# Layer 1's projections with norm statistics and one sine table in PSUM, and tokens normed in places of their own

## The chip, the core and the metric

The kernel runs on one core of a Trainium2 chip. Its engines work side by side, each through its own instruction queue in order: TensorE (PE in the profile; PEld is its weight load) multiplies and transposes, VectorE (DVE) and ScalarE (ACT) work element by element and can read and write PSUM, GpSimd (POOL) works on SBUF only, and SyncE (SP) issues most of the DMAs. The metric is the device time of one execution in microseconds.

## What is computed

Two layers over 2048 tokens of width 1024, all in float32. Layer 0 is a mixer with two kinds of banded attention. The change is in layer 1 (and in when one preparation for it is done):

```python
def odd_layer(x, norm_g, w_in, w_out, qn, kn, lq1, lk1, lq2, lk2, subln_g, cos, sin, lambda_init):
    h = rms_norm(x, norm_g)
    proj = h @ w_in
    q, k, v, gate = jnp.split(proj, [C_QK, 2 * C_QK, 2 * C_QK + C_W], axis=-1)
    q = rms_norm(q.reshape(b, s, C_HEADS, 2, HEAD_DIM), qn)
    k = rms_norm(k.reshape(b, s, C_HEADS, 2, HEAD_DIM), kn)
    q1 = apply_rope(q[:, :, :, 0], cos, sin)
...
    o = differential_attention(q1, q2, k1, k2, v, lam)
    o = rms_norm(o, subln_g) * (1.0 - lambda_init)
    y = (o.reshape(b, s, C_W) * jax.nn.silu(gate)) @ w_out
    return x + y
```

`rms_norm` divides by the root of the mean square and multiplies by a gain; `apply_rope` turns each head's two halves of 32 by an angle that depends on the position.

## The kernel before

A float32 product is made of three matmuls: each factor is split into a high part (a ScalarE copy to the matmul's rounded type) and a low part (the remainder, by VectorE or GpSimd), and high x high, high x low and low x high are added in PSUM (names ending in H and L).

`project1` makes queries, keys and values of layer 1 by quarters, with seven products of 256 x 256 squares in place of eight. `PRODUCTS` names them: some multiply quarters of the hidden tokens with quarters of the weights, others sums of quarters (s1 to s4 of the tokens, and sums of the weights that `weight_sums` made while layer 0 ran and stored in the DRAM tensor `t`). Three PSUM accumulators per block hold them: X runs through products 0, 2, 3 and 4 and is copied out after each (tiles a, b, c, d of the pool `xp`), Y holds product 1, Z products 5 and 6; VectorE adds Y and Z to the copied tiles.

The tokens come in two halves of two blocks of 512 (blocks 3 and 2, then 0 and 1). In each half run six groups of 512 columns: values, two of queries, two of keys, values. `steps` gives the order in a group: 14 steps, seven products for each of two blocks (`bi` 0 and 1). In query and key groups both blocks follow each other within a product; in value groups block 1 trails by `LAG` products. A step is 2 x 4 x 3 = 24 matmuls (L759).

Around a step:
- `operand` (L511 to L518) loads one square of weights (`ws`, L514), splits it on ScalarE (L516) and GpSimd (L517) into places of `wp`; `fetch` calls it ahead of use, `gate_weights` eight more times for the gate.
- `hidden` (L536 to L606) is a generator that makes a block: for each of two pairs of token tiles it loads them (L550), squares (L552), takes the inverse root with `rstd` (L197 to L210), scales (L556), transposes on TensorE (L562), splits and adds the quarters (L566 to L599). Tokens, their raw sums and the tiles a to d share the places of the tag `x`.
- `normed` (L627 to L649) norms one quarter of queries or keys of both blocks: squares on ScalarE (L631), a sum on VectorE (L633), `rstd` (ScalarE's Ln and Exp at L204 and L205, four small VectorE operations at L206 to L209), a product (L635), the two sine products on VectorE (L641), and the cosine product and the sum on GpSimd (L645, L649).
- `turn` (L651 to L661) transposes a normed quarter (L656), empties it from PSUM on ScalarE (L658) and VectorE (L659) and stores both parts. Eight turns of a group are spread over the following steps by `later` and `tick`.
- `tables` (L616 to L625) loads cosines and sines of the half's positions and multiplies them with the gains by `rope_tables` (L177 to L195), four tables in SBUF.

The places: PSUM has eight banks, two for transposes (`ptr`) and six for products (`pmm`). In SBUF there are 8 places for weight parts (four pairs), 3 each for the two split results (`ep`), and 6 for `x`. The program's order is a priority: the order of each engine's queue is fixed at build time by a scheduler that plays the program through a model of the engines and takes what is ready first, so an instruction can stand in its queue far ahead of its place in the program.

At the start of the first half the whole of block 3 is made before the first step, block 2 beside the first steps (the generator is advanced after steps of block 0 in group 0). At the change of halves the first new block is begun after the last step of `bi` 0 in the last group, the second beside the next group's first steps.

In layer 0, `project0` runs a round of `weight_sums` per block and group, from the second group of the first half on: a load, four GpSimd operations (L463) and a store, 24 rounds.

Of the kernel before, what the change touches and what calls it, by code (L numbers as in the profile page):

```python
# [10 lines left out]
F32 = mybir.dt.float32  # L11
F32R = mybir.dt.float32r
AF = mybir.ActivationFunctionType
# [19 lines left out]
def f32(ap):  # L33
    return ap.bitcast(F32)
# [52 lines left out]
class Trunk:  # L87
# [88 lines left out]

    def rope_tables(self, pool, gain, scale, tag, nt=S // P):  # L177
        nc = self.nc
        C = pool.tile([P, nt, HD], F32, tag=tag + "C", name=tag + "C")
        Sn = pool.tile([P, nt, HD], F32, tag=tag + "S", name=tag + "S")  # L180

# [43 lines left out]
    def project0(self, es):  # L225
# [166 lines left out]
        for half in range(2):  # L392
# [12 lines left out]
            for gi, (kind, c0, width, o) in enumerate(groups):  # L405
# [4 lines left out]
                for bi, b in enumerate(blocks):  # L410
                    if half or gi:
                        next(sums, None)
# [72 lines left out]
    def project1(self, es):  # L485
# [12 lines left out]
        tq = pool("tq", 2)  # L498
        ep = pool("e", 3)
        sums[0][1] = pool("s1a", 1)  # L500
        gn = pool("g", 1)
        st = pool("st", 3)
        wp = pool("w", 8)
        sums[0][4] = pool("s4a", 1)
        xp = pool("x", 6)
        ptr = pool("ptr", 2, space=PSUM)
        pmm = pool("pmm", 6, space=PSUM)
        mm = nc.tensor.matmul
# [25 lines left out]
        nc.sync.dma_start(gain, a["od_norm"].to_broadcast([P, D]))  # L534

        def hidden(b, i, h):  # L536

# [6 lines left out]

            for p in range(2):
                xs, ss = [], sm.tile([P, 2], F32, tag="xss", name=n + "xss")
                for e in range(2):
                    t = b * NTB + 2 * e + p
                    xt = xp.tile([P, D], F32, tag="x", name=n + "xt")
                    nc.sync.dma_start(xt, x[t * P:(t + 1) * P, :])  # L550
                    junk = tq.tile([P, D], F32, tag="tq", name=n + "junk")
                    nc.scalar.activation(junk, xt, AF.Square, accum_out=ss[:, e:e + 1])  # L552
                    xs.append(xt)
                r = self.rstd(sm, ss, 2, 1.0 / D, n + "x")
                for e in range(2):
                    nc.vector.scalar_tensor_tensor(xs[e], xs[e], r[:, e:e + 1], gain, ALU.mult, ALU.mult)  # L556

                def turned(e, q):
# [11 lines left out]
                def of(k, part):  # L570
                    return S_[k]["HL".index(part)][:, :, p * P:(p + 1) * P]
# [25 lines left out]
                for k in (2, 3, 1, 4):  # L597
                    nc.scalar.activation(of(k, "H"), raws[k], AF.Copy)
                    nc.gpsimd.tensor_tensor(of(k, "L"), raws[k], f32(of(k, "H")), ALU.subtract)  # L599
                yield  # L600
            if b:
# [14 lines left out]
        def tables(blocks):  # L616
# [6 lines left out]
            self.cos, self.sin = (t.rearrange("p r b j d -> p (r b j) d") for t in (cos, sin))  # L623
            tabs["q"] = self.rope_tables(tb, self.gain["od_q_norm"], 0.125, n + "tq", 8)
            tabs["k"] = self.rope_tables(tb, self.gain["od_k_norm"], 1.0, n + "tk", 8)  # L625

        def normed(C, r, tab):  # L627
# [3 lines left out]
            nc.scalar.activation(sq, C.rearrange("p t c -> p (t c)"), AF.Square)  # L631
            ss = sm.tile([P, 16], F32, tag="qss", name=n + "qss")
            nc.vector.tensor_reduce(ss, sq.rearrange("p (h d) -> p h d", d=HD), AX.X, ALU.add)  # L633
            rs = self.rstd(sm, ss, 16, 1.0 / HD, n + "q")
            nc.vector.tensor_tensor(v, v, rs.unsqueeze(2).to_broadcast([P, 16, HD]), ALU.mult)  # L635
# [31 lines left out]
        halves_ = [(3, 2), (0, 1)]  # L667
        LAG = 2

# [34 lines left out]
        h = [{}, {}]  # L704
        making = [hidden(halves_[0][0], 0, h[0]), hidden(halves_[0][1], 1, h[1])]
        for _ in making[0]:
            pass
        making = making[1:]
        tables(halves_[0])
        for _ in range(3):  # L710
            fetch()

        for half, blocks in enumerate(halves_):
            for gi, (kind, g, o) in enumerate(groups):
                T, ps, done = {}, {}, set()
                if kind == "qk":
                    next(gates, None)

                def tile_(nm):
# [24 lines left out]
                for si, (p, bi) in enumerate(steps(half, gi)):  # L744
# [7 lines left out]
                    if opens:  # L752
                        ps[bank, bi] = pmm.tile([P, 2, Q], F32, tag="mm", name=n + "mm" + bank)
                    acc = ps[bank, bi]
# [34 lines left out]
                    tick()  # L789
                    if half == 0 and gi == len(groups) - 1 and bi == 0 and p == self.ORDERS[0][-1]:  # L790
                        nxt = [{}, {}]
                        making = [hidden(halves_[1][i], i, nxt[i]) for i in range(2)]
                        next(making[0])
                    elif half == 0 and gi == len(groups) - 1 and len(making) == 2:
                        next(making[0], None)
                    if gi == 0 and bi == 0 and making:
                        if next(making[0], 0) == 0:
                            making.pop(0)
                if half == 0 and gi == len(groups) - 1:
                    for _ in making.pop(0):  # L800
                        pass
                    h = nxt
                    tables(halves_[1])
        while later:
# [787 lines left out]
```

## Time and profile before

| | us |
|---|---|
| median of three executions | 2926.62 |
| lowest and highest | 2919.79 and 2930.2 |
| the profiled execution | 2917.79 |
| its span, first to last instruction | 2916.0 |

All durations are from the profiled execution. In its views a row of a stretch has its bounds, its length, busy time and number of instructions of each engine, the granted TensorE clock (1.00 is full), and the DMA share with GB/s. A row of a group has line, engine, operation, output and inputs, shapes and count, then busy us and mean ns, then the idle time before and what ended it. A row of waits has total us, number and longest. A row of the timeline has start, duration, engine and line. The page in 40 slices of 73 us (busy tenths; layer 1's projections are slices 17 to 26):

```profile
PE   6999999999899999697978998899999999999998
DVE  8763285347778773449863787359887787776772
POOL 6764254335445454367755777336676666777661
PEclk9999999999999999799998999999999999999999
```

### The profile page before, as it was taken

Reading aid. Unit: us, or ns where it says so; the run is one execution under the profiler, and the core shown is the slowest. Engines: PE = TensorE matmul, PEld = TensorE weight load, DVE = VectorE, ACT = ScalarE, POOL = GpSimd, SP = SyncE. Lnnn points to the kernel's source line nnn. Section 1 sums busy time; section 2 is a strip of 40 time slices with the busy share of each in tenths; the row PEclk is TensorE's granted clock in tenths of the full one; section 3 lists DMA queues with packets and bytes.
Section 4 is the critical chain, followed back from the end, with each engine's and each line's share of the span. In section 5 each row is a group of like instructions: output and inputs, shape, how many; then the busy total and the mean of one; then the engine's idle time right before and its main releaser. Section 6 shows DMA issues by size and latency. Waiting matters only on the chain. (4 is left out here: it accounts for less than half of the span.)

```text
span 2916.0 us, 47395 instructions
## 1 busy us (share of the span) xinstructions
PE 2696.0 (92%) x15112; PEld 2248.2 (77%) x15112; DVE 1933.4 (66%) x4436; ACT 1680.0 (58%) x4011; POOL 1651.3 (57%) x1603
## 2 busy tenths in 40 slices
PE   6999999999899999697978998899999999999998
PEld 5788887888788888597977998677676777676676
DVE  8763285347778773449863787359887787776772
ACT  4443544367767673443434444458897787776761
POOL 6764254335445454367755777336676666777661
PEclk9999999999999999799998999999999999999999
DMA  7897348737877675455655455997868675555442
GB/s 227 288 329 252 110 153 269 236 114 236 234 203 193 181 201 163 156 180 157 203 197 174 152 188 190 236 265 196 242 194 232 183 227 183 141 174 146 145 152 91
DMA packets 420521, 568.03 MB, mean 195 GB/s; under 512 B 44720, under 2 KB 219568, under 8 KB 420272
## 3 DMA queue, kind: packets, MB, share of 16 engines
q1 hardware_dynamic: 411568, 556.61, 63.3%
q10 hardware_dynamic: 8704, 8.39, 0.9%
q8 instruction: 120, 1.97, 0.3%
q14 instruction: 129, 1.06, 0.1%
HBM read 394.21 MB, written 170.66 MB: 194 GB/s over the span
## 5 line engine op out<-in xcount | busy, mean ns | idle before, releaser
L1247 ACT ACTIVATE cP<-cS,cnm 128x512 f32<-128x512 f32 (+3 forms) x640 | 393.8, 620 | 146.4 <-DVE cnm L1244 119.3
L1244 DVE TENSOR_REDUCE cnm<-cS 128x1 f32<-128x512 f32 (+3 forms) x640 | 373.9, 601 | 50.7 <-PE cS L1241 44.2
L1280 POOL TENSOR_TENSOR cP<-cP,cP 128x512 f32<-128x512 f32 (+1 forms) x320 | 356.8, 1143 | 30.8 <-ACT cP L1278 29.7
L1279 POOL TENSOR_SCALAR cP<-cP,crl,cel 128x512 f32<-128x512 f32 (+3 forms) x288 | 206.7, 730 | 239.6 <-DVE crl L1261 134.2
L1296 PE MATMUL cO<-cpt,cv 128*128 128x512 f32 (+3 forms) x640 | 290.7, 541 | 5.9 <-DVE cpt L1294 4.4
L517 POOL TENSOR_TENSOR p1wL<-p1ws,p1wH 128x1024 fp32r<-128x1024 f32 x92 | 227.4, 2476 | 104.2 <-ACT p1wH L516 94.6
L1240 PE MATMUL cS<-ck,cqd 128*128 128x512 f32 (+3 forms) x640 | 262.7, 414 | 14.8 <-DMA ck<-kH 6.4
L1294 DVE COPY cpt<-ctr 128x512 f32<-128x512 f32 (+1 forms) x320 | 190.8, 605 | 121.0 <-PE ctr L1292 118.1
L292 POOL TENSOR_TENSOR p0wL<-p0ws,p0wH 128x512 fp32r<-128x512 f32 (+1 forms) x140 | 170.6, 1244 | 170.8 <-ACT p0wH L290 162.2
L215 PE MATMUL p0mm<-p0wH,p0hH 128*128 128x512 f32 (+1 forms) x640 | 238.9, 376 | 8.6 <-ACT p0vt L447 7.2
L217 PE MATMUL p0mm<-p0wH,p0hL 128*128 128x512 f32 (+1 forms) x640 | 238.6, 373 | 2.8 <-DVE p0hL L318 2.8
L216 PE MATMUL p0mm<-p0wL,p0hH 128*128 128x512 f32 (+1 forms) x640 | 238.3, 373 | 0.0
L1241 PE MATMUL cS<-ck,cql 128*128 128x512 f32 (+3 forms) x640 | 232.5, 368 | 2.0 <-DMA cql<-qL 2.0
L1292 PEld LDWEIGHTS ctr<-ident,cP 128*128 128x128 f32 x1088 | 138.8, 142 | 120.2 <-issue 63.7
L1278 ACT ACTIVATE cP<-cP,cc 128x512 f32<-128x512 f32 (+1 forms) x320 | 189.4, 651 | 26.1 <-DVE cc L1264 24.9
L1292 PE MATMUL ctr<-ident,cP 128*128 128x128 f32 x1088 | 176.9, 276 | 4.1 <-ACT csq L1325 2.6
L759 PE MATMUL p1mmX<-p1wH,p1hH 128*128 128x256 f32 x576 | 168.1, 292 | 8.6 <-ACT p1hH L567 6.1
L516 ACT ACTIVATE p1wH<-p1ws 128x1024 fp32r<-128x1024 f32 x92 | 96.4, 1056 | 125.8 <-PE p1mmX L759 48.7
L759 PE MATMUL p1mmX<-p1wH,p1hL 128*128 128x256 f32 x576 | 166.2, 289 | 0.0
L759 PE MATMUL p1mmX<-p1wL,p1hH 128*128 128x256 f32 x576 | 166.2, 289 | 0.0
L1240 PEld LDWEIGHTS cS<-ck,cqd 128*128 128x128 f32 x640 | 122.1, 191 | 46.3 <-ACT cP L1247 16.3
L215 PEld LDWEIGHTS p0mm<-p0wH,p0hH 128*128 128x128 f32 x640 | 121.3, 190 | 31.0 <-ACT p0vt L447 9.5
(374 smaller groups left out, 8465.8 us busy)
## 6 DMA issues: line engine op xcount, KB each, us to landing
p0ws<-in_ev_w_in_dram SPq DMA_DIRECT2D x48, 512.0 KB, 5.5
p1ws<-t SPq DMA_DIRECT2D x48, 512.0 KB, 4.4
p1ws<-in_od_w_in_dram SPq DMA_DIRECT2D x44, 512.0 KB, 4.4
ck<-kH SPq DMA_DIRECT2D x144, 128.0 KB, 3.6
ck<-kL SPq DMA_DIRECT2D x144, 128.0 KB, 3.8
cv<-v SPq DMA_DIRECT2D x72, 256.0 KB, 4.1
cwH<-wgH SPq DMA_DIRECT2D x64, 256.0 KB, 5.4
cwL<-wgL SPq DMA_DIRECT2D x64, 256.0 KB, 5.8
```

What stands on the lines that cost most here:

```text
L215: mm(ps, aH, bH, start=first, stop=False)
L216: mm(ps, aH, bL, start=False, stop=False)
L217: mm(ps, aL, bH, start=False, stop=last)
L517: nc.gpsimd.tensor_tensor(L, ws, f32(H), ALU.subtract)
L759: mm(acc[:, pr, :], l, r_[:, k, :], start=opens and pr == k == i == 0, stop=k == 3 and i == 2, skip_group_check=True,)
L1240: mm(ps, qd[:, m, js], kt[:, :wd], start=True, stop=False)
L1241: self.anchor = mm(ps, ql[:, m, js], kt[:, :wd], start=False, stop=True).ins
L1244: nc.vector.tensor_reduce(nm[:, m, z:z + 1], ps, AX.X, ALU.max, negate=True)
L1247: exp = nc.scalar.activation(chunks[z][:, :wd], ps, AF.Exp, bias=nm[:, m, z:z + 1], accum_out=acc).ins
L1280: nc.gpsimd.tensor_tensor(p1, p1, p2, ALU.add)
L1292: nc.tensor.transpose(turned[:, (j - j0) * P:(j - j0 + 1) * P], us[j][kt // 4][:, kk:kk + P], self.ident)
L1296: mm(O[:, j0 * P:], v, T[:, :wd], start=(kt == 0), stop=(kt == nkt - 1), skip_group_check=True)
```

## The change

Seven edits in layer 1's projections and one in layer 0's:

1. `root` replaces `rstd` there. Sum, two intermediates and result of a norm lie in one PSUM tile with eight turns (bank `pst`); three VectorE operations in place of four. Ln and Exp stay on ScalarE, their results in SBUF.
2. `table` makes the tables of one kind when the first group that needs them begins; the sine table goes to one PSUM bank (`ptb`) that queries and keys share in turn, the cosine tables stay in SBUF.
3. `pmm` has two banks for X and two that Y and Z share, in place of six.
4. `hidden` loads, squares and scales a pair in `load`, in four places of their own (`hx`), and transposes it in `turn_pair`. Both pairs can be loaded before the first is transposed.
5. A table `todo` says after which step of which group the generators go on: the first block of the second half is loaded after step 3 of the last group and transposed after steps 12 and 13.
6. `LAG` is 1 in place of 2.
7. Places: `wp` 6 (three pairs) in place of 8, `ep` 2 in place of 3, `xp` 5 in place of 6. Two fetches of weights instead of three stand ahead of the first step.
8. `project0` takes two rounds of `weight_sums` per block and group, in its second half only.

```diff
-    def rope_tables(self, pool, gain, scale, tag, nt=S // P):
+    def rope_tables(self, pool, gain, scale, tag, nt=S // P, other=None, to=None):
...
-        Sn = pool.tile([P, nt, HD], F32, tag=tag + "S", name=tag + "S")
+        Sn = (other or pool).tile([P, nt, HD], F32, tag=to or tag + "S", name=tag + "S")
...
-                    if half or gi:
+                    if half:
+                        next(sums, None)
                         next(sums, None)
...
-        ep = pool("e", 3)
+        ep = pool("e", 2)
...
-        wp = pool("w", 8)
+        wp = pool("w", 6)
         sums[0][4] = pool("s4a", 1)
-        xp = pool("x", 6)
+        hx = pool("hx", 4)
+        xp = pool("x", 5)
         ptr = pool("ptr", 2, space=PSUM)
-        pmm = pool("pmm", 6, space=PSUM)
+        ptb = pool("ptb", 1, space=PSUM)
+        pst = pool("pst", 1, space=PSUM)
+        pmm = pool("pmm", 2, space=PSUM)
...
+        stats = pst.tile([P, 8, 3, 16], F32, tag="st", name=n + "st")
+        turns = [0]
+
+        def root(m, scale):
+
+            at = stats[:, turns[0] % 8, :, :m]
+            turns[0] += 1
+            ss, u, rs = (at[:, i, :] for i in range(3))
+
+            def finish():
+                ln, y = (sm.tile([P, m], F32, tag=f"{nm}{m}", name=n + nm) for nm in ("ln", "y0"))
+                nc.scalar.activation(ln, ss, AF.Ln, bias=self.eps, scale=scale)
+                nc.scalar.activation(y, ln, AF.Exp, scale=-0.5)
+                stt = nc.vector.scalar_tensor_tensor
+                stt(u, ss, EPS / scale, y, ALU.add, ALU.mult)
+                stt(u, u, -0.5 * scale, y, ALU.mult, ALU.mult)
+                stt(rs, u, 1.5, y, ALU.add, ALU.mult)
+                return rs
+
+            return ss, finish
...
-            for p in range(2):
-                xs, ss = [], sm.tile([P, 2], F32, tag="xss", name=n + "xss")
+            def load(p):
+                xs, (ss, finish) = [], root(2, 1.0 / D)
                 for e in range(2):
                     t = b * NTB + 2 * e + p
-                    xt = xp.tile([P, D], F32, tag="x", name=n + "xt")
+                    xt = hx.tile([P, D], F32, tag="hx", name=n + "xt")
                     nc.sync.dma_start(xt, x[t * P:(t + 1) * P, :])
                     junk = tq.tile([P, D], F32, tag="tq", name=n + "junk")
                     nc.scalar.activation(junk, xt, AF.Square, accum_out=ss[:, e:e + 1])
                     xs.append(xt)
-                r = self.rstd(sm, ss, 2, 1.0 / D, n + "x")
+                r = finish()
                 for e in range(2):
                     nc.vector.scalar_tensor_tensor(xs[e], xs[e], r[:, e:e + 1], gain, ALU.mult, ALU.mult)
+                return xs
+
+            def turn_pair(p, xs):
...
+            loaded = []
+            for p in range(2):
+                loaded.append(load(p))
+                yield
+            for p in range(2):
+                turn_pair(p, loaded[p])
                 yield
...
-            tabs["q"] = self.rope_tables(tb, self.gain["od_q_norm"], 0.125, n + "tq", 8)
-            tabs["k"] = self.rope_tables(tb, self.gain["od_k_norm"], 1.0, n + "tk", 8)
+
+        def table(nm):
+            tabs[nm] = self.rope_tables(
+                tb, self.gain[f"od_{nm}_norm"], 0.125 if nm == "q" else 1.0, n + "t" + nm, 8, ptb, n + "sin"
+            )
...
-            ss = sm.tile([P, 16], F32, tag="qss", name=n + "qss")
+            ss, finish = root(16, 1.0 / HD)
             nc.vector.tensor_reduce(ss, sq.rearrange("p (h d) -> p h d", d=HD), AX.X, ALU.add)
-            rs = self.rstd(sm, ss, 16, 1.0 / HD, n + "q")
+            rs = finish()
...
-        LAG = 2
+        LAG = 1
...
+        first, second = (hidden(b, i, h[i]) for i, b in enumerate(halves_[0]))
+        next(first)
+        next(first)
+        for _ in range(2):
+            fetch()
+        next(first)
+        next(second)
+        next(first)
+        next(second)
         tables(halves_[0])
-        for _ in range(3):
-            fetch()
+        todo = {}
+        todo[0, 0, 1] = [second]
+        todo[0, 0, 2] = [second]
+        todo[0, 0, 4] = [first]
+        todo[0, 0, 8] = [second]
+        nxt = [{}, {}]
+        first, second = (hidden(b, i, nxt[i]) for i, b in enumerate(halves_[1]))
+        last_group = len(groups) - 1
+        todo[0, last_group, 3] = [first, first]
+        todo[0, last_group, 12] = [first, second]
+        todo[0, last_group, 13] = [first, second]
+        todo[1, 0, 1] = [second]
+        todo[1, 0, 2] = [second]
+        todo[1, 0, 8] = [first, second]
...
                 if kind == "qk":
                     next(gates, None)
+                    if o["tab"] != groups[gi - 1][2].get("tab"):
+                        table(o["tab"])
...
-                        ps[bank, bi] = pmm.tile([P, 2, Q], F32, tag="mm", name=n + "mm" + bank)
+                        ps[bank, bi] = pmm.tile([P, 2, Q], F32, tag="x" if bank == "X" else "yz", name=n + "mm" + bank)
...
+                    for made in todo.get((half, gi, si + 1), ()):
+                        next(made, None)
+            h = nxt
+            if half == 0:
+                tables(halves_[1])
```

More of the change, by code (lines that the diff above doesn't have):

```diff
@@ L704, in project1 @@
         h = [{}, {}]
[L705 to L708, printed above, removed]
-        tables(halves_[0])
-        for _ in range(3):
-            fetch()
+        first, second = (hidden(b, i, h[i]) for i, b in enumerate(halves_[0]))
[7 more added lines that the diff above has]
+        next(second)
+        tables(halves_[0])
+        todo = {}
[12 more added lines that the diff above has]
+        todo[1, 0, 8] = [first, second]
         for half, blocks in enumerate(halves_):
@@ L789, in project1 @@
                     tick()
[L790 to L803, printed above, removed]
+                    for made in todo.get((half, gi, si + 1), ()):
[3 more added lines that the diff above has]
+                tables(halves_[1])
         while later:
```

## The prediction

> **What bounds the kernel now.** First the page, then busy time by stretches of layer 1's projections (L759 runs from 1176 to 1840 us), then the waits of TensorE, then the groups of the engine that they name. The page says only that TensorE is busy 92%:
>
> ```profile
> PE 2696.0 (92%) x15112; PEld 2248.2 (77%) x15112; DVE 1933.4 (66%) x4436; ACT 1680.0 (58%) x4011; POOL 1651.3 (57%) x1603
> ```
>
> The stretches of L759 alone (length, PE and weight-load busy with counts, granted clock, DMA), one undisturbed stretch of all engines for the rate, and the same stretches of the transposes, two of L656 and two of L562:
>
> ```profile
> 1176.00:1240.00 64.00, 26.67 (x160) 25.02 (x161) 0.71 0.52 166
> 1240.00:1320.00 80.00, 79.81 (x662) 79.31 (x662) 1.00 0.56 172
> 1320.00:1520.00 200.00, 157.75 (x1199) 151.90 (x1197) 0.91 0.58 184
> 1520.00:1580.00 60.00, 30.12 (x203) 28.24 (x204) 0.80 0.48 157
> 1580.00:1640.00 60.00, 60.00 (x499) 59.69 (x498) 1.00 0.58 182
> 1640.00:1840.00 200.00, 168.66 (x1319) 162.74 (x1317) 0.96 0.60 191
> ...
> 1260.00:1280.00 20.00, 20.00 (x169) 20.00 (x168) 6.97 (x10) 8.74 (x12) 11.92 (x6) 1.00 0.66 197
> ...
> 1320.00:1520.00 200.00, 21.97 (x120) 16.14 (x120) 0.91 0.58 184
> 1640.00:1840.00 200.00, 21.68 (x124) 15.84 (x124) 0.96 0.60 191
> ...
> 1176.00:1240.00 64.00, 11.11 (x54) 8.16 (x52) 0.71 0.52 166
> 1520.00:1580.00 60.00, 11.76 (x63) 8.75 (x60) 0.80 0.48 157
> ```
>
> At 169 products in 20 us one takes 0.1183 us. Length less count times 0.1183, less the transposes' weight loads (8.2 us in the first stretch, 16.1 in the third, 8.8 in the fourth, 15.8 in the last), is the time lost: 64 - 18.9 - 8.2 = **36.9** us at the start, 200 - 141.8 - 16.1 = **42.1**, 60 - 24.0 - 8.8 = **27.2** at the change of halves, 200 - 156.0 - 15.8 = **28.2**, and about 1 us in the two stretches between. Together 135 us, of which part is the low clock (0.71, 0.80, 0.91) that follows each gap. What TensorE waits for in this stage:
>
> ```profile
> PE p1trq L656 <- DVE p1eL L659: 45.0, 7, 10.1
> ...
> PE p1trh L562 <- DVE p1xt L556: 38.6, 6, 11.6
> ```
>
> The 45.0 us lie in the query and key groups (third and sixth stretch): a transpose needs a PSUM place that VectorE has yet to empty. The 38.6 us lie at the start and the change of halves. Why VectorE is late there is in its groups from 1176 to 1840 us (busy, mean ns), and in the min/median/max of two lines:
>
> ```profile
> L208 DVE TENSOR_TENSOR p1qu<-p1qu,p1qms 128x16 f32<-128x16 f32 x32 | 50.4, 1575 | 1.1
> L659 DVE TENSOR_TENSOR p1eL<-p1trq,p1eH 128x512 fp32r<-128x512 f32 x64 | 42.2, 684 | 29.9 <-ACT p1eH L658 24.0 <-DMA qL<-p1eL 4.0 <-DMA kL<-p1eL 1.1
> L206 DVE TENSOR_SCALAR p1qms<-p1qss 128x16 f32<-128x16 f32 x32 | 30.5, 953 | 0.8
> L207 DVE SCALAR_TENSOR_TENSOR p1qu<-p1qy 128x16 f32<-128x16 f32 x32 | 26.8, 836 | 1.8 <-ACT p1qy L205 1.7
> L635 DVE TENSOR_TENSOR p1cb<-p1cb,p1qr 128x1024 f32<-128x1024 f32 x8 | 21.6, 2706 | 0.2
> L209 DVE SCALAR_TENSOR_TENSOR p1qr<-p1qu,p1qy 128x16 f32<-128x16 f32 x32 | 18.5, 579 | 1.1
> L635 DVE TENSOR_TENSOR p1ca<-p1ca,p1qr 128x1024 f32<-128x1024 f32 x8 | 9.8, 1224 | 0.2
> ...
> L208 DVE TENSOR_TENSOR p1qu<-p1qu,p1qms x32: 174/2268/2360, 1277.9 to 1804.2; 128x16 f32<-128x16 f32 x32
> ...
> L659 DVE TENSOR_TENSOR p1eL<-p1trq,p1eH x64: 674/682/695, 1327.2 to 1823.7; 128x512 fp32r<-128x512 f32 x64
> ```
>
> Sixteen elements take 0.17 us or 2.3 us, while 512 elements from PSUM never take more than 0.695. The timeline inside the longest gap (1373.8 to 1384.0 us) shows with what the slow ones go:
>
> ```profile
> 1376.87 2.56 DVE L189 TENSOR_TENSOR p1tqS<-p1sin,od_q_norm 128x256 f32<-128x256 f32 x1
> 1379.35 2.42 DVE L192 TENSOR_SCALAR p1tqS<-p1tqS 128x256 f32<-128x256 f32 x1
> ...
> 1376.63 2.51 POOL L517 TENSOR_TENSOR p1wL<-p1ws,p1wH 128x1024 fp32r<-128x1024 f32 x1
> 1379.11 2.51 POOL L649 TENSOR_TENSOR p1cb<-p1cb,p1t 128x1024 f32<-128x1024 f32 x1
> ...
> 1383.96 0.69 PE L656 MATMUL p1trq<-ident,p1ca 128*128 128x128 f32 x2 [10.13 <-DVE p1eL L659]
> ```
>
> A VectorE operation that has all its tensors in SBUF stands until the GpSimd operation begun before it ends. The 128 small ones cost 126.2 us where 128 x 0.174 = 22.3 would do: 104 us, and L635 on cb 12 more. That is 116 us of VectorE's time, in an order where the emptying of PSUM queues behind it.
>
> **The change part by part.**
> *Statistics and sine in PSUM.* The sum, the two intermediates and the result of each norm now lie in PSUM, and each of the three small operations left (one of four goes, 32 x 0.95 = 30.5 us with it) has one PSUM operand; L635 and the rope products L641 have one too. I take the standing as gone for them, by the nearest row (L659: one PSUM and one SBUF input, 64 times, 674 to 695 ns). What no row here shows is VectorE writing to PSUM: bounds 0.17 us (L208 unhindered) and 0.69 (L659 whole) for a small one; at the upper end 96 x 0.5 = 50 us return to an engine that has 116 free, so the path doesn't see it. The norm's cosine table and the building of both sine tables still read two SBUF operands. The two sine tables share one place, so the key table is written between the last query norm and the first key norm: four operations of up to 2.5 us, 5 us of gap in each half, 10 in all (bounds 0 and 2 x 10.1, the longest gap today).
>
> On the shared read port, the Trainium skill (SBUF — State Buffer, Who interferes with whom) says that a VectorE instruction with at most one SBUF input doesn't contend outside the two-port modes. By it the writes to PSUM that no row shows are free as well; the first rival below would then have 0.05 instead of its 0.10.
>
> *Fewer PSUM banks* (6 to 4 for products; Y and Z share two). Z opens three steps after Y closes, 3 x 24 x 0.1183 = 8.5 us for VectorE to empty it; with the standing gone I cost this at nothing. If VectorE stays as late as in the longest gap (10.1 us), 1.6 us show in each opening.
>
> *Tokens in places of their own.* Today the second load of a block is issued only when the first pair has been worked through, and the chain load, square, root, scaling is open:
>
> ```profile
> 1175.26 0.39 PE L217 MATMUL mom<-mw,myL 128*128 128x512 f32 x1
> ...
> 1176.78 0.92 SPq L550 DMA_DIRECT2D p1xt<-x  x2
> 1198.33 2.62 SPq L550 DMA_DIRECT2D p1xt<-x  x2
> ...
> 1187.83 2.48 DVE L556 SCALAR_TENSOR_TENSOR p1xt<-p1xt,p1xr,p1g_in 128x1024 f32<-128x1024 f32 x2
> ```
>
> From issue to scaled it takes 1176.8 to 1190.3 = 13.5 us. With four places both pairs of the first block are scaled under layer 0's last matmuls (the last ends at 1175.6), and at the change of halves under the last value group. The second block still loads when the places come free, some 2.5 us after the first transposes, so about 16 us late, its second pair some 6 us later. Beside that stand four pairs' transposes (8 us) and three to four products of 2.84: 17 to 19 of 23 us. I leave 14 us lost at the start (clock included) and 8 at the change, where two more products (5.7 us) run meanwhile: gains **23** and **19**. LAG 1 instead of 2 brings the second block's first product one step (2.84 us) forward; it is in these.
>
> *Three weight places, two for the split results, five for tokens.* What these lean on:
>
> ```profile
> L517 POOL TENSOR_TENSOR p1wL<-p1ws,p1wH 128x1024 fp32r<-128x1024 f32 x88 | 217.9, 2480 | 96.5 <-ACT p1wH L516 94.0 <-PE p1mmX L759 2.3
> L649 POOL TENSOR_TENSOR p1cc<-p1cc,p1t 128x1024 f32<-128x1024 f32 x8 | 19.3, 2406 | 0.3
> L516 ACT ACTIVATE p1wH<-p1ws 128x1024 fp32r<-128x1024 f32 x88 | 92.1, 1056 | 118.7 <-PE p1mmX L759 48.7 <-PE p1mmZ L759 38.1 <-POOL p1wL L517 20.0
> ...
> SPq L514 <- POOL p1wL L517: 213.0, 56, 8.0
> ...
> qL<-p1eL SPq DMA_DIRECT2D x32, 256.0 KB, 3.7
> ```
>
> A product of both blocks takes 48 x 0.1183 = 5.7 us. A pair made in a freed place has two products, 11.4 us, instead of three, 17.0. It needs 1.06 + 2.48 = 3.5 us, so 7.9 are left for GpSimd's queue, in which two norms are 4 x 2.4 = 9.6. Split results have two turns, about 6.6 us, to be emptied and stored (1.3 + 3.7 to land), on a queue that waits 213 us for weights. Bounds: 0, and 1.8 us twice in eight groups plus as much again for stores and clock, about 55. I take 1 us in each of 12 groups, **12**, since the queue is rarely that full; LAG and five places I hide behind the same steps.
>
> *Weight sums later.* They are taken up as soon as their places allow, not where the program has them:
>
> ```profile
> L463 POOL TENSOR_TENSOR p0ts<-p0ts x96: 720/737/1719, 25.6 to 286.9; 128x256 f32<-128x256 f32 x96
> ...
> PE p0trh L313 <- DVE p0xt L308: 18.8, 5, 12.9
> ```
>
> Their loads and stores move with them, past SP's weight loads. I take 0; bounds 10 gained (half of the opening's 18.8 us) and 10 lost where they crowd the second half.
>
> *Sum.* The two long stretches lose 70.3; left are 10 (sine), 12 (places) and 4 of low clock behind them: gain **44**. 23 + 19 + 44 = **86 us**. The profiled execution took 2917.8 us (span 2916.0), so 2831.8 by it. The median of the three runs, 2926.6, is 8.8 above; I set the same gain against it: 2840.6, forecast **2840**.
>
> **The rivals.**
> *VectorE stays late* (writing PSUM costs, or the sine hand-over holds it): only the start and the change gain, 42 us, 2885. For it: no row shows the write; against: the 64 emptyings of L659, with one operand in PSUM, never stand.
> *The loads still come late* (SP is in order and waits 213 us for weights): only 44, 2883.
> *Nearly all of the loss goes*: 135 less the second blocks' 15 = 120, 2807. For it: 1240 to 1320 us, where 662 products fill the time.
> *Slower: GpSimd.* In a query or key group it has 8 x 2.48 + 8 x 2.4 = 39.0 us beside 14 x 2.84 + 32 x 0.13 = 43.9 of TensorE. If each of the 84 products waits for its weights, the change loses from 86 / 84 = 1.02 us each; at 1.3, 84 x 1.3 - 86 = 23 slower, 2950. For it: the third place has no reserve for two norms in a row; against: no product waits for weights today.
>
> *One bank for all statistics.* If ScalarE must stand while VectorE works on another turn of the same tile, the logarithm of each norm waits for the product of the one before (L635, 1.22 us), with the weight copies of L516 behind it: 32 x 1.22 = 39 us of ScalarE. It has room (81.6 of 200 us busy in the third stretch), so half of that at most reaches TensorE: 2860.
>
> ```profile
> 1320.00:1520.00 200.00, 167.64 (x1323) 166.23 (x1322) 160.11 (x172) 81.63 (x132) 131.75 (x55) 0.91 0.58 184
> ```
>
> That is the rule of the Trainium skill (PSUM — Partial Sum Buffer, PSUM bank collisions raise a hardware error): two engines may touch one bank only one after the other, whatever the columns. No run here shows it yet.
>
> **How the numbers follow.** Forecast 0.55, VectorE late 0.10, loads late 0.09, nearly all 0.10, one bank 0.07, GpSimd 0.05, hardly any gain 0.04. Within 0.3% (9 us, about what a measurement here can tell from none) lies most of the last, 0.03; slower by more is GpSimd with the rest of it, 0.06; the others, 0.91, are faster. The bounds (places 0 to 55, sine 0 to 20, sums 10 either way) and the rivals up to one bank give 2803 to 2889.
>
> **What would show it.** Right: the small VectorE operations near 0.2 us, L659's wait by TensorE under 15 us, loads of the first block before the last layer 0 matmul, clock above 0.95 in the long stretches. Wrong: products waiting for L517, ScalarE or VectorE waiting for stores of split results, a gap of 10 us before the second block.

## The result, and the profile after

| | before | after |
|---|---|---|
| median, us (four executions each) | 2928.41 | 2843.73 |
| lowest and highest | 2919.79 and 2933.24 | 2839.35 and 2847.77 |
| the profiled execution | 2917.79 | 2839.35 |
| its span | 2916.0 | 2837.5 |

The ratio is 0.9714 (95% interval 0.9686 to 0.9741): 84.7 us faster by the medians, against a forecast of 2840. Lines have moved: the products L759 are now L816, the transposes L656 L694, their emptying L659 L697, the head transposes L562 L590, the product L635 L673, the scaling L556 L581.

The page of the kernel after, engines and slices (rows that answer to those shown of before):

```profile
PE 2680.5 (94%) x15112; PEld 2234.1 (79%) x15112; DVE 1795.5 (63%) x4396; ACT 1672.6 (59%) x4011; POOL 1657.4 (58%) x1603
...
PE   6899999999899999799998998999999999999998
...
DVE  8763186337777775335663563468887887777762
...
PEclk9999999999999999999999999999999999999999
```

VectorE is busy 138 us less (1933.4 before), and the two slices with a clock of 7 and 8, at the start of the stage and at its change of halves, are gone. The products L816 by stretches, then the transposes L590 in the first and third and L694 in the second, third and last (length, PE and weight-load busy with counts, clock, DMA share, GB/s):

```profile
1176.00:1240.00 64.00, 33.47 (x206) 31.34 (x207) 0.79 0.72 229
1240.00:1460.00 220.00, 210.60 (x1684) 205.02 (x1684) 0.99 0.61 190
1460.00:1520.00 60.00, 41.55 (x301) 37.92 (x301) 0.97 0.73 231
...
1580.00:1755.00 175.00, 165.56 (x1316) 159.55 (x1315) 1.00 0.70 218
...
1176.00:1240.00 64.00, 13.05 (x64) 9.71 (x64) 0.79 0.72 229
1460.00:1520.00 60.00, 9.98 (x64) 7.42 (x64) 0.97 0.73 231
...
1240.00:1460.00 220.00, 18.71 (x120) 13.92 (x120) 0.99 0.61 190
1460.00:1520.00 60.00, 1.25 (x8) 0.88 (x8) 0.97 0.73 231
1580.00:1755.00 175.00, 19.07 (x126) 14.32 (x126) 1.00 0.70 218
```

By the prediction's own reckoning (length less products at 0.1183 us less the transposes' weight loads) the time lost is now: start 64 - 24.4 - 9.7 = 29.9 us (36.9 before), query and key groups 220 - 199.2 - 13.9 = 6.9 and 175 - 155.7 - 14.3 = 5.0 (42.1 and 28.2 before), change of halves 60 - 35.6 - 8.3 = 16.1 (27.2 before). So the groups gained **58** us, the start only **7**, the change **11**: 76 in all. (These stretches have round bounds; from matmul to matmul the whole is 80.7 us shorter, as the experiments below count it.) What TensorE waits for from 1100 to 1800 us:

```profile
PE p1trh L590 <- DVE p1xt L581: 14.9, 5, 7.1
...
PE p1trq L694 <- DVE p1eL L697: 5.3, 7, 1.3
...
PE p1mmZ L816 <- ACT p1wH L520: 0.9, 1, 0.9
```

The 45.0 us on the emptied transposes have become 5.3, with none above 1.3 us, and products wait for weights once (0.9 us). VectorE's groups show why (busy, mean ns; 1170 to 1780 us):

```profile
L697 DVE TENSOR_TENSOR p1eL<-p1trq,p1eH 128x512 fp32r<-128x512 f32 x64 | 42.9, 688 | 56.6 <-ACT p1eH L696 26.1 <-DMA kL<-p1eL 16.7 <-DMA qL<-p1eL 12.6
...
L581 DVE SCALAR_TENSOR_TENSOR p1xt<-p1xt,p1st,p1g_in 128x1024 f32<-128x1024 f32 x16 | 28.1, 1793 | 0.3
...
L673 DVE TENSOR_TENSOR p1cb<-p1cb,p1st 128x1024 f32<-128x1024 f32 x8 | 9.7, 1218 | 0.2
L555 DVE SCALAR_TENSOR_TENSOR p1st<-p1st,p1y 128x16 f32<-128x16 f32 (+1 forms) x40 | 7.1, 178 | 1.2
...
L189 DVE TENSOR_TENSOR p1tkS<-p1sin,od_k_norm 128x256 f32<-128x256 f32 x2 | 5.0, 2500 | 0.1
```

A small operation that reads one input from PSUM and writes PSUM takes 178 ns (579 to 1575 before), and the product on cb 1218 instead of 2706. What still reads two tensors from SBUF still stands: the scaling L581, and the building of the key's sine table L189, although its result now lies in PSUM.

The start did not do what was forecast. ScalarE's timeline of the kernel after, then TensorE's last product of layer 0 and the first transposes of layer 1:

```profile
1137.89 1.06 ACT L577 ACTIVATE p1junk<-p1xt 128x1024 f32<-128x1024 f32 x1 [1.68 <-DMA p1xt<-x]
...
1139.25 1.06 ACT L577 ACTIVATE p1junk<-p1xt 128x1024 f32<-128x1024 f32 x1 [0.24 <-DMA p1xt<-x]
...
1180.12 0.26 ACT L551 ACTIVATE p1ln<-p1st,eps 128x2 f32<-128x2 f32 x1 [29.32 <-DMA x<-mxr]
...
1176.34 0.39 PE L217 MATMUL mom<-mw,myL 128*128 128x512 f32 x1
1183.86 1.97 PE L590 MATMUL p1trh<-ident,p1xt 128*128 128x128 f32 x8 [7.13 <-DVE p1xt L581]
```

The first pair is loaded and squared by 1140 us, well under layer 0. Then its logarithm stands until 1180, released by the last store of layer 0's output tile `mxr`. The logarithm reads nothing of layer 0. Its small output tile, however, comes from the pool `sm`; a first reading was that, with two sine tables fewer in SBUF ahead of it, this pool lies on the place of the `mxr` tiles. The kernel before did not have this wait: there the same logarithm ran at 1140.9 us, and its pair was scaled and transposed at once behind layer 0:

```profile
1142.81 2.48 DVE L556 SCALAR_TENSOR_TENSOR p1xt<-p1xt,p1xr,p1g_in 128x1024 f32<-128x1024 f32 x2
...
1175.49 0.71 PE L562 MATMUL p1trh<-ident,p1xt 128*128 128x128 f32 x5
```

The first product followed layer 0's last matmul after 1.3 us before, and follows it after 11.7 us now: at this point the change lost what the kernel before already had, and the 7 us gained at the start are the balance.

### The profile page after: what moved, and what is told of

Same layout as the page of the kernel before. It is cut to its first block, busy times and chain, and to the rows that moved or that the text cites. A ratio compares the mean times of both kernels' runs of the same rounds, so it can differ in the third digit from the quotient of the medians.

```text
span 2837.5 us, 47396 instructions
## 1 busy us (share of the span) xinstructions
PE 2680.5 (94%) x15112; PEld 2234.1 (79%) x15112; DVE 1795.5 (63%) x4396; ACT 1672.6 (59%) x4011; POOL 1657.4 (58%) x1603
## 4 chain that ended last, share of the span: by engine, by line
PE 64%; DMA 8%; DVE 5%; ACT 3%; issue 2%; SPq 1%; POOL 1%; ACTq 0%; DVEq 0%; POOLq 0%
PE p1mmX L816 8%; PE cO L1344 8%; PE cS L1288 4%; PE p1mmZ L816 4%; PE cS L1289 4%; PE ctr L1340 4%; PE p1mmY L816 2%; PE com L215 2%; PE com L216 2%; PE com L217 2%; PE mom L215 2%; PE mom L216 2%; PE mom L217 2%; PE mtrB L1113 2%; PE cG L215 1%
## 5 line engine op out<-in xcount | busy, mean ns | idle before, releaser
L1292 DVE TENSOR_REDUCE cnm<-cS 128x1 f32<-128x512 f32 (+3 forms) x640 | 374.8, 602 | 55.3 <-PE cS L1289 48.5
L1328 POOL TENSOR_TENSOR cP<-cP,cP 128x512 f32<-128x512 f32 (+1 forms) x320 | 357.9, 1145 | 35.2 <-ACT cP L1326 34.7
L1326 ACT ACTIVATE cP<-cP,cc 128x512 f32<-128x512 f32 (+1 forms) x320 | 189.0, 651 | 21.4 <-DVE cc L1312 20.7
L816 PE MATMUL p1mmX<-p1wH,p1hH 128*128 128x256 f32 x576 | 167.7, 291 | 7.3 <-ACT p1hH L595 5.3
L816 PE MATMUL p1mmX<-p1wH,p1hL 128*128 128x256 f32 x576 | 166.1, 288 | 0.0
L816 PE MATMUL p1mmX<-p1wL,p1hH 128*128 128x256 f32 x576 | 165.6, 287 | 0.0
```

The lines of the kernel that those rows point to most:

```text
L816: mm(acc[:, pr, :], l, r_[:, k, :], start=opens and pr == k == i == 0, stop=k == 3 and i == 2, skip_group_check=True,)
L1292: nc.vector.tensor_reduce(nm[:, m, z:z + 1], ps, AX.X, ALU.max, negate=True)
L1328: nc.gpsimd.tensor_tensor(p1, p1, p2, ALU.add)
```

## The experiments

Two things are compared throughout: the time against the kernel before on the same chip, and, from the profile, the **stage**, from the end of layer 0's last matmul to the end of layer 1's last product. The stage leaves out layer 0, which hardly any edit touches and which ended anywhere from 1175.7 to 1186.5 us in the fourteen profiles. But each stage is that of a single profile: seven weight places and the early weight sums, whose medians are within 1 us of the kernel after, have stages 3.7 and 5.4 us longer, so a difference of that size says little. Stage: 664.2 us before (1175.65 to 1839.81), 583.5 after (1176.73 to 1760.22), 80.7 shorter.

| kernel | median, us | before beside it | ratio, 95% | stage, us |
|---|---|---|---|---|
| after | 2843.73 | 2928.41 | 0.9714 (0.9686 to 0.9741) | 583.5 |
| statistics in SBUF | 2883.67 | 2924.06 | 0.9854 (0.9830 to 0.9878) | 618.7 |
| sine table in SBUF | 2865.17 | 2924.06 | 0.9795 (0.9778 to 0.9813) | 604.9 |
| both in SBUF | 2901.25 | 2924.06 | 0.9919 (0.9899 to 0.9939) | 641.1 |
| before, with the PSUM places alone | 2867.02 | 2926.78 | 0.9793 (0.9771 to 0.9814) | 607.1 |
| LAG 2 | 2855.56 | 2926.78 | 0.9756 (0.9738 to 0.9773) | 596.4 |
| three split results | 2838.70 | 2926.78 | 0.9699 (0.9679 to 0.9719) | 578.5 |
| seven weight places | 2844.55 | 2923.08 | 0.9730 (0.9715 to 0.9745) | 587.2 |
| weight sums early | 2844.28 | 2926.78 | 0.9721 (0.9702 to 0.9739) | 588.9 |
| small tiles moved | 2840.33 | 2924.06 | 0.9709 (0.9688 to 0.9731) | 571.9 |
| first pair's small tiles moved | 2826.63 | 2923.08 | 0.9671 (0.9657 to 0.9685) | 567.3 |
| all moved, three split results | 2833.76 | 2923.08 | 0.9681 (0.9661 to 0.9702) | 570.4 |
| first moved, three split results | 2819.34 | 2923.08 | 0.9641 (0.9621 to 0.9660) | 560.3 |

Cut where its twelve groups of 336 products end, the stage shows where an edit acts. The first group holds the start, the seventh the change of halves:

| kernel | first group, us | seventh, us | the ten others, us |
|---|---|---|---|
| before | 85.7 | 76.4 | 502.1 |
| after | 79.1 | 60.6 | 443.8 |
| both in SBUF | 75.5 | 60.4 | 505.2 |
| before, with the PSUM places alone | 84.5 | 78.4 | 444.2 |
| LAG 2 | 81.7 | 65.4 | 449.3 |
| small tiles moved | 66.5 | 63.4 | 442.0 |
| first pair's small tiles moved | 69.1 | 63.0 | 435.3 |

**Is it the placement? Statistics, sine, both back in SBUF.** Everything else as after.

```diff
-        pst = pool("pst", 1, space=PSUM)
+        pst = pool("pst", 1)
```

> The changed kernel with one edit: the statistics tile of the norms lies in SBUF again (sine table, banks, places and order as changed). Theory A (VectorE's all-SBUF operations stand behind GpSimd's): the three small operations of the 32 norms are back at 0.6 to 1.6 us in the mean instead of 0.17 to 0.18, some 79 us of VectorE, the product with the root on the last quarter near 2.7 us; TensorE's wait for the split results goes from 5.3 us to 30 to 45, and the time from 2844 to 2880 to 2900 us. Rival B (the gain in the query and key groups comes from the new places and order, not from where the statistics lie): 2840 to 2850 us, and TensorE's wait stays under 10 us.

```diff
-        ptb = pool("ptb", 1, space=PSUM)
+        ptb = pool("ptb", 1)
```

> The changed kernel with the shared sine table in SBUF (statistics stay in PSUM). Theory A: the 64 sine products, 0.68 us each now, stand in part again, up to the 19 us that they cost more before; VectorE has room for that, so TensorE sees at most 10 us: 2844 to 2854 us. Rival B: no difference, neither in these products nor in the time.

> The changed kernel with both the statistics and the shared sine table in SBUF: what is left of the change are the places for tokens, the order, the shared banks, the three weight places. Theory A: 2885 to 2910 us, that is about the 58 us back that the query and key groups gained, and TensorE's wait for the split results near the 45 us of before. Rival B: 2840 to 2855 us.

The stage grows by 35.2, 21.4 and 57.6 us: the two parts add up. With the statistics in SBUF, two of VectorE's groups and TensorE's longest rows of waits:

```profile
L555 DVE SCALAR_TENSOR_TENSOR p1st<-p1st,p1y 128x16 f32<-128x16 f32 (+1 forms) x40 | 37.0, 928 | 1.2
...
L673 DVE TENSOR_TENSOR p1cb<-p1cb,p1st 128x1024 f32<-128x1024 f32 x8 | 25.9, 3244 | 0.2
```

```profile
PE p1mmZ L816 <- DVE p1ca L825: 13.2, 6, 2.4
...
PE p1trq L694 <- DVE p1eL L697: 8.6, 4, 3.8
```

The standing is back and the time, 2884, is in the range of theory A, but the wait is not where I looked for it: only 8.6 us on the emptied transposes, where 30 to 45 were expected, and 18.1 with both in SBUF, where 45 were. A late VectorE now shows first where Z opens in a bank that Y has to leave (13.2 us, at most 2.4 each time; the prediction had 1.6 for this case). The sine table alone cost 21 us, more than either theory had; the means of its eight groups of products go from 682 to 684 ns up to 1070 to 2302.

**The same from the other side: the kernel before with the PSUM places alone** (with its banks, its three small operations and its tables made when they are needed, and the small tiles kept off `mxr`; lines are those of this run: L585 are the head transposes, L682 the others).

> The kernel before with one edit carried over: norm statistics and sine table in PSUM (so four banks for products and three small operations in a norm), the small SBUF tiles opened after s3 so that they keep off layer 0's x tiles; loads, order, LAG, 8/3/6 places as before. Theory A (the placement gives about 57 us of the 84 by itself, the places and the order the rest): 2862 to 2882, TensorE's wait for the emptying of the query and key transposes under 15 us, small VectorE operations 0.17 to 0.18 us. Theory B (the placement pays only together with tokens normed ahead): above 2892. Theory C (the placement is all of it): 2840 to 2854.

Its stage is 607.1, 57.1 shorter than before. Its waits by TensorE:

```profile
PE p1trh L585 <- DVE p1xt L579: 37.1, 6, 11.2
...
PE p1trq L682 <- DVE p1eL L685: 3.5, 3, 1.3
```

The 45.0 are gone and the 38.6 at the start and the change are not: each edit has its own stretches, as the table of the groups shows from both sides. The placement alone takes the ten other groups from 502.1 to 444.2 us and leaves the first and the seventh as they were; without it (both in SBUF) the first and the seventh gain and the ten others do not. Of 80.7 us some 57 are the placement, and about 24 the order and the places.

**LAG.**

```diff
-        LAG = 1
+        LAG = 2
```

> The kernel after with LAG 2 again. Theory A (the order of the value groups hides nothing at present, since the second block is late by its own loads): within 4 us of the kernel after, ratio to the kernel before 0.970 to 0.973. Theory B (LAG 1 brings the second block one step of 2.84 us forward at the start and at the change): 5 to 8 us slower, ratio 0.973 to 0.9745.

Both theories were too low: the stage is 12.9 us longer, with the wait for scaled tokens 23.3 us (14.9 with LAG 1):

```profile
PE p1trh L590 <- DVE p1xt L581: 23.3, 5, 7.1
```

By the groups, 2.6 us of it lie in the first and 4.8 in the seventh, where the prediction had 2.84 for each; the other 5.5 lie in the ten others, where it had none.

**The places.** `ep = pool("e", 3)`; and, apart from it, `wp = pool("w", 7)`.

> The kernel after with three places for each split result in place of two. Theory A (VectorE and ScalarE wait 44 us in all for the stores of split results, but TensorE waits only 5.3 us for the emptied transposes, so that the wait is hidden): 0 to 5 us faster, ratio 0.9697 to 0.9714, and the waits of VectorE for the stores under 5 us. Theory B (the 12 us that the prediction left for the places are there): 9 to 14 us faster, ratio 0.9665 to 0.9683.

> The kernel after with seven places for weight parts in place of six. Theory A (products wait 0.9 us for weights in the whole stage, so three pairs suffice): within 4 us of the kernel after, ratio 0.970 to 0.973. Theory B (the 12 us that the prediction left for the places lie in the weights): 4 to 9 us faster, ratio 0.9685 to 0.970.

With three split results the stage is 5.0 us shorter, which alone says little, and the time is 5 us lower, but the intervals of the ratios overlap. VectorE's waits for its stores fall from 29.3 us to 14.8, not below 5 as expected:

```profile
DVE p1eL L697 <- DMA kL<-p1eL: 7.8, 3, 4.5
DVE p1eL L697 <- DMA qL<-p1eL: 7.0, 3, 3.4
```

A seventh weight place gains nothing.

**Weight sums.** One round per block and group from the second group on, as before.

> The kernel after with one round of weight sums per block and group from the second group on, as in the kernel before. Theory A (they lie in gaps of GpSimd either way): within 4 us of the kernel after, ratio 0.970 to 0.973. Theory B (later sums keep the queues of the opening free, or crowd the second half): more than 5 us either way, below 0.9697 or above 0.9731.

No difference that the intervals can tell.

**The start.** The pool `sm` is opened behind `s3a` instead of ahead of it.

> The changed kernel with one line moved: the pool of the small norm tiles (logarithm and its exponential) is opened after the place of the token sum s3 instead of before it. Theory S: in the changed kernel these tiles lie where layer 0's last output tiles lie (four KB of tables fewer stand below them), so the first block's logarithm waits for the last store (1180.1 us, 40 us after its squares); moved, it runs at 1141 us, both pairs are scaled before layer 0's last matmul, the gap of 7.1 us before the first transposes goes and with it some low clock: 8 to 14 us less, 2830 to 2836 us. Rival R (the one bank for statistics, or the order of the queues, holds the norms back): the logarithm still runs after 1175 us and the time is 2840 to 2848 us.

The mechanism is confirmed: nothing but the places of `sm` and of one token sum change, and the first logarithm runs at 1143.3 instead of 1180.1 us; the first product comes 1.2 us after layer 0's last matmul. The first group is 12.6 us shorter and the stage 11.6, yet the median is only 3 us lower, in the rival's range. Part of it was taken back at the end of layer 0, whose last 200 output matmuls take 60.7 us instead of 55.3 (55.1 to 57.3 in the seven other runs that hold the first pair). VectorE and TensorE there:

```profile
1154.97 5.12 DVE L581 SCALAR_TENSOR_TENSOR p1xt<-p1xt,p1st,p1g_in 128x1024 f32<-128x1024 f32 x2
1160.02 1.27 DVE L872 TENSOR_TENSOR mxr<-mom,mxr 128x512 f32<-128x512 f32 x2
...
1156.46 0.66 PE L590 MATMUL p1trh<-ident,p1xt 128*128 128x128 f32 x4 [0.25 <-ACT p1r L609]
1160.75 0.79 PE L215 MATMUL mom<-mw,myH 128*128 128x512 f32 x1 [3.64 <-DVE mxr L872]
1161.34 0.63 PE L216 MATMUL mom<-mw,myH 128*128 128x512 f32 x1
```

The second pair's scalings, fixed in VectorE's queue ahead of layer 0's additions L872, take 5.12 us for two (the first pair's had taken 2.49), and layer 0's matmuls wait 3.64 us for a PSUM place, then run for some 5 us at one per 0.43 us instead of 0.23 (the granted clock from 1160 to 1166 us is 0.53). Freeing one wait had put other work ahead of layer 0's. So the next edit frees the first pair alone:

```diff
+        sm0 = pool("sm0", 1)
...
+            own = sm0 if turns[0] == 1 else sm
...
-                ln, y = (sm.tile(
+                ln, y = (own.tile(
```

> The kernel after with a place of its own for the small tiles of the very first pair's root alone; all others stay where they slid. Theory S2 (the held root of the first pair costs about 12 us between layer 0's last matmul and 1240 us, and moving both pairs gave some 5 us back because two scalings stood ahead of layer 0's last evacuations): the first pair is scaled by 1150 us, the second still after 1180, TensorE's wait for mxr near 0.6 us, 5 to 11 us faster than the kernel after, ratio to the kernel before 0.9675 to 0.9697. Rival (the second pair, still held, costs what the first gains): ratio 0.9705 to 0.972.

It is 17 us faster than after by the medians, more than the 5 to 11 expected, and the intervals of the ratios just do not meet (0.9685 and 0.9686). The stage is 16.2 us shorter, but only 10.0 of it lie in the first group. Another 6.6 lie in six of the ten others (the query groups and the second key group of each half) that have nothing to do with the first pair: there TensorE's products themselves come faster, at the same granted clock. The products in the same 20 us, in the kernel after and in this run:

```profile
1260.00:1280.00 20.00, 20.00 (x169) 20.00 (x168) 1.00 0.65 193
...
1260.00:1280.00 20.00, 20.00 (x178) 20.00 (x177) 1.00 0.53 160
```

Their starts are 0.120 us apart in the kernel after, as in all twelve kernels without `sm0`, and 0.113 to 0.118 in most of this run and of the next one, the only two with `sm0`. It is not the chip, since two of the twelve ran on the same one as these. The pool also moves every SBUF pool that is opened behind it; whether that is the reason was not tested.

One expectation failed: TensorE's wait for `mxr` is 3.6 us in three times, as in the kernel after (3.5), since there it is the loads of `mxr` that are late; but the 3.64 behind the scalings is gone. Against the run with all small tiles moved, the profiled spans differ by 8.1 us: 4.0 at the end of layer 0, where the last 200 output matmuls take 56.7 us (1.3 us less waiting, 12 x 0.2 = 2.4 less of low clock), and 4.6 in the stage, where the first group is 2.6 us longer than in that run and the faster products make more than that good. The medians differ by 14; the rest was not traced.

**Both gains together.**

> The edit of the run before together with three places for the split results. If both gains are real and independent: 8 to 15 us faster than the kernel after, ratio 0.966 to 0.969, the time 2828 to 2836. If they are the same microseconds: as the better of the two.

> All small tiles moved off layer 0's x tiles, and three places for the split results. If the gains add: 4 to 9 us faster than the kernel after, ratio 0.968 to 0.970; slower than the run with the first pair alone by about 5 us, if the two scalings ahead of layer 0's evacuations are what gave the gain back.

With the first pair alone they add, and to more than the 8 to 15 us expected: 2819.34 us, the ratio 0.9641 (0.9621 to 0.9660), the fastest here and 24 us below the kernel after. Six of its groups too have the faster products, worth 6 us against the run with three split results alone. With all small tiles moved it is 2833.76 us, 10 below the kernel after, and 14 above this one where about 5 were expected. The three pairs of runs with and without the third place differ by 5, 7 and 7 us in their medians and by 5.0, 1.5 and 7.0 in the stage, so a gain of some 5 us is likely, though none of the pairs has intervals that stay apart. TensorE's waits in the fastest (its lines are three further on: L593 are the head transposes, L697 the others):

```profile
PE p1trh L593 <- DVE p1xt L584: 6.2, 3, 3.1
...
PE p1trq L697 <- DVE p1eL L700: 4.0, 4, 1.5
```

## Why the prediction was right, and where it was not

The time came within 4 us of the forecast because one term was too small (44, gained 58) and two were too large (23 and 19, gained 7 and 11). The mechanism of the largest term is shown from both sides; that the errors of the three nearly cancel is luck. The prediction's 0.1183 us for a product is a little short: the 169 products in 20 us include those begun before, and their starts are 0.120 apart, which takes some 2 us from the time lost in each long stretch and changes none of this.

- **Standing goes with one operand in PSUM: right.** 0.178 us for the small operations, 1.22 for L673 and 0.68 for the rope products. The write to PSUM, which no row had shown, costs nothing (bounds had been 0.17 and 0.69). The rule of the Trainium skill (SBUF — State Buffer, Who interferes with whom), by which a VectorE instruction with at most one SBUF input does not contend outside the two-port modes, agrees with these 0.178 us. With two SBUF inputs L555 takes 0.928 us on average (statistics in SBUF).
- **Query and key groups, 44 forecast, 58 gained.** The 26 us left standing were the error: 10 for the sine hand-over, 12 for three weight places and two split results, 4 for the clock. 11.9 us are lost there in all. No wait for an emptied transpose exceeds 1.3 us, though the key table is built between the last query norm and the first key norm with operations of 2.5 us. The first key groups of the two halves take 48.1 and 45.0 us where the second take 43.8, so the hand-over costs at most 5.5 us of its 10, and part of these are stores (46.6 and 44.1 with three split results). Of the 12, split results are some 5 us and weights nothing. The sign of being wrong "VectorE waiting for stores of split results" did show, 29.3 us of it, but the wait of TensorE behind it is the 5.3 us.
- **Start, 23 forecast, 7 gained.** The step that failed is "both pairs of the first block are scaled under layer 0's last matmuls". They were loaded there; the scaling waited for a place. I had followed the transfers and the queues and not where the small tiles come to lie when two tables leave the pool ahead of them. It put at nothing what can hold the scaling, and so did not see that the change would take away the early first pair that the kernel before had. With all small tiles moved both pairs are scaled there, as forecast, and the first group is 12.6 us shorter: 6.6 + 12.6 = 19.2 of the 23. The price, 5.4 us at the end of layer 0, was in no term.
- **Change of halves, 19 forecast, 11 gained.** The mechanism was right: both pairs were loaded ahead, and the first block was transposed between the last products. Mis-sized was what is left: 16.1 us instead of 8, in single waits of up to 2.7 us for scaled tokens and for ScalarE's copies.
- **LAG 1**, counted within those two terms as one step of 2.84 us each, is worth 2.6 and 4.8 us there, and 12.9 us of stage in all. Its term was mis-sized by what it gives elsewhere.
- **Fewer banks, 0: right**, and so was its condition: with VectorE late again (statistics in SBUF) the openings of Z cost 13.2 us.
- **Weight sums, 0: right** within what can be told.

Of the rivals, *VectorE stays late* falls with the 178 ns; *GpSimd* falls since a product waits for weights only once, 0.9 us, and a seventh place gains nothing; *the loads come late* falls by the squares at 1138 us. *Nearly all of the loss goes* was wrong as a forecast, but the fastest version, at 2819, comes within 12 us of its 2807, though 6 us of that are the faster products, which no term had. *One bank for all statistics* was not tested: each of the 18 logarithms from 1240 to 1460 us follows its own sum, and none of the 40 in the stage lies beside a VectorE operation on another turn, so there was nothing that could have stood; the time speaks against its 2860. The rule of the Trainium skill that it rests on (PSUM — Partial Sum Buffer, PSUM bank collisions raise a hardware error) is neither shown nor contradicted by these runs.

## What to carry to other kernels

Where small VectorE operations take ten times their length in step with GpSimd, let each read one of its inputs from PSUM: here 57 us, and the cost of a bank was nothing as long as VectorE was on time. A result in PSUM alone did not help: L189, with both inputs in SBUF, takes 2.5 us. When a change frees SBUF, look at which later tiles slide onto places of the stage before: a tile of a few bytes can hold a whole chain, and the row that shows it is a wait for a transfer that the instruction has no business with. Before freeing such a chain, look at what stands behind it in the in-order queue: all of it freed shortened the first group by 12.6 us and lengthened the end of layer 0 by 5.4; its first part alone gave 10.0 for 1.4, and 1.4 is within the scatter. And before giving a gain to an edit, look whether the parts that it does not touch still run at their old pace: here 6.6 of 16.2 us did not belong to the tile that was moved.

## What the runs showed that was not expected

The products that come 0.113 us apart instead of 0.120 at a granted clock of 1.00, in the two runs with one more small pool, are the largest open end. With the statistics in SBUF again, L673 on cb took 3.24 us on average, more than the 2.71 of the kernel before; why more was not traced. A scalar in PSUM does not help where both tensors are in SBUF: L581 still took 1.79 us on average, and 2.6 each in the pair at 1155 us of the run with all small tiles moved. And a stop of TensorE can be paid twice: in that run, after 3.64 us of waiting, the next eleven matmuls came 0.43 us or more apart instead of 0.23. The length of the stop alone does not decide it: after 2.25 us at the same place in the kernel after they came 0.23 to 0.24 apart from the second on, but with seven weight places, after 2.25 us as well, seven of them came 0.43 apart.
